# Bringing the first half chunk of x in whole float32 rows on the hardware DMA queues, in a matmul with a decayed running sum

## The chip, the cores and the metric

One core of a Trainium2 chip runs the kernel. The metric is the device time of one execution in microseconds. The core has TensorE (matmuls, "PE" in the profile, its weight loads "PEld"), VectorE (DVE), ScalarE (ACT), GpSimd (POOL) and SyncE (SP). SP and ACT issue DMAs on hardware queues (q1 and q10 in the profile's lists), GpSimd on a software queue (q0). A DMA on GpSimd's queue can change float32 to bfloat16 on the way; here every load on it does.

## The reference

```python
B, S, D = (16, 2048, 1024)      # x is B x S x D, w is D x D, decay has D entries, all float32
xw = x @ w
out[:, 0, :] = xw[:, 0, :]
for t in range(1, S):
    out[:, t, :] = decay[None, :] * out[:, t - 1, :] + xw[:, t, :]
```

It is a matmul of 32768 rows by 1024 x 1024, and then for each of the 1024 output columns a first-order recurrence along time.

## The kernel before

x is cut into 64 chunks of 512 time steps (`TL`), two of which make a group. x has its time steps on rows, while the matmul needs the contracted index on partitions, so each chunk is loaded as bfloat16, turned in blocks of 32 x 32 pairs on VectorE (`turn`, L115), and its even and odd entries are separated by a copy (`part`, L123). The 1024 contracted indices fall into 8 sets k = 2m + e of 128: m from 0 to 3, and e, which says whether the even or the odd entries of x's pairs are meant. Even k can be multiplied straight from the turned pairs (`xw`); odd k take the separated copy (`xt`). For a group, TensorE (`matmul`, L131) computes 8 column tiles n of 128 columns into PSUM; ScalarE, GpSimd and VectorE do the recurrence, VectorE turns the result back (L272) and SP stores it.

The order on every engine is written out by hand: `pin` keeps instructions in program order, and the strings in `agenda` name the work, a letter and a number each. All that the change touches is in the opening, `agenda[-99]`, and in the first matmuls (`step == 0`, L583 to L602). The opening's letters, before the change:

- M0, M1, M2, M3: loads of half chunks of x (chunk 0, first and second half of 256 time steps, then chunk 1), four DMAs each on GpSimd's queue (L105). They are called x0, x1, x2 and x3 below.
- w comes in four quarters, each four DMAs of 32 partitions (`load_w`, L313): the even k of the first 512 columns on SP's and ACT's queues at the very start ("w00"), then on GpSimd's queue U0, the odd k of the same columns ("w01"), and U1 and U2, the same for the other 512 columns.
- W and w, 0 to 15: `settle_one`, the copy of one m of such a quarter from where it landed (`stage`) into the weights `wsb` (L320), W on VectorE and w on ScalarE. 0 to 3 are w00, 4 to 7 are w01.
- E0 to E3: the turns of x0, one m each, on VectorE; E4 to E7 those of x1; E8 to E15 chunk 1's.
- F and G, numbered like E: the separating copies, F on VectorE, G on ScalarE.
- D: the decay values, loaded by SP, turned and squared on VectorE (L367 to L373).
- K0 to K3 and `spin`: matmuls whose result nobody reads. `spin(22, ...)` runs 22 of them from the start; K0 to K3 each copy one element of a landed quarter of x0 into a small tile `gates` on ScalarE (L354) and then run 3, 3, 3 and 2 more with that tile as weights, so that they can't start before the data is there.
- L: a load of a later chunk.

After the opening, step 0 multiplies chunk 0 by the first four column tiles: first the even k of x0 for all four (16 matmuls of 256 columns, k by k), then the even k of x1 (16 more), then the odd k over all 512 columns (16 matmuls), then chunk 1 (the loops from L594). The results lie in `heads`, three PSUM tiles of two banks, whose first banks are `firsts` and second banks `seconds`; `spare` and `spare1` are the fourth pair.

Before chunk 0's results exist, two of the output tiles (`room`) are free, and w's quarters land in them (`stage`, L306).

Of the kernel before, what the change touches and what calls it, by code (L numbers as in the profile page):

```python
# [10 lines left out]
BF16 = mybir.dt.bfloat16  # L11
ALU = mybir.AluOpType


def _ap(ap_obj: bass.AP, new_ap, extra_offset=0):
    return dataclasses.replace(
        ap_obj,
        ap=[list(p) for p in new_ap],
        offset=ap_obj.offset + extra_offset,
    )  # L20
# [5 lines left out]
def kernel(  # L26
# [26 lines left out]
    nc = tc.nc  # L53
    pin = tc.keep_in_program_order
    B, S, D = x.shape
    assert w.shape == (D, D)

    NQ = 4
    P = 32
    CQ = D // NQ  # L60
    K = CQ // P
    M = K // 2
    TL = 512
    NJ = TL // P
    NC = S // TL
    R = K // 2
# [3 lines left out]
    const = ctx.enter_context(tc.tile_pool(name="const", bufs=1))  # L70
    sb = ctx.enter_context(tc.tile_pool(name="sb", bufs=1))
# [4 lines left out]
    def ring(pool, name, count, shape, dtype=FP32):  # L76
        i = turns[name] = turns.get(name, -1) + 1
        return pool.tile(shape, dtype, name=f"{name}{i % count}")

    def quad(q):  # L80
        return slice(q * P, (q + 1) * P)
# [15 lines left out]
    xb_of = {}  # L97
    xw_of = {}
    xt_of = {}
# [25 lines left out]
    def matmul(ps, n, k, xt, t0=0, t1=TL, start=0, pairs=None):  # L125
        if pairs is None:
            rhs = xt[:, k // 2, k % 2, t0:t1]
        else:
            rhs = pairs[:, k // 2, t0 // P:t1 // P, :, k % 2].rearrange("p j i -> p (j i)")
        lhs = wsb[:, k, n].rearrange("p q i -> p (q i)")  # L130
        pin(nc.tensor.matmul(  # L131
            out=ps[:, t0:t1] if ps.shape[1] >= t1 else ps,
            lhsT=lhs,
            rhs=rhs,
            start=(k == 0 and t0 == start),
            stop=(k == K - 1),
        ))
# [3 lines left out]
    class Tile:  # L141
# [39 lines left out]
        def copy(self):  # L181
            self.xs = sb.tile([128, 2 * TL], FP32, name=f"xs{self.lot % 3}")[:, 0:self.T]
            parts = self.ps if isinstance(self.ps, tuple) else (self.ps,)
            size = self.T // len(parts)
            for i, ps in enumerate(parts):
                pin(nc.scalar.copy(out=self.xs[:, i * size:(i + 1) * size], in_=ps))  # L186
# [118 lines left out]
    size = M * CH  # L305
# [5 lines left out]
    def load_w(queues, h, e):  # L311
        for i, q in enumerate((0, 2, 1, 3)):
            pin(queues[i % len(queues)].dma_start(  # L313
                out=stage[h, e][quad(q)].rearrange("p (m d) -> p m d", m=M),
                in_=_ap(w, [[2 * D, P], [2 * P * D, M], [1, CH]],
                        (q * CQ + e) * D + h * CH)))
# [7 lines left out]
    spare = ring(psp, "spare", 1, [128, TL])  # L324
    rows = const.tile([128, 2, P], FP32, name="rows")
    touch = const.tile([128, 1], BF16, name="touch")
    load_w((nc.sync, nc.scalar), 0, 0)
    pin(nc.vector.memset(idle, 0.0))  # L328
    pin(nc.vector.memset(rows, 0.0))
    pin(nc.scalar.copy(out=touch, in_=idle[:, 0:1]))  # L330

    gates = [const.tile([128, 128], BF16, name=f"gate{q}") for q in range(NQ)]
    for gate in gates:
        pin(nc.vector.memset(gate, 0.0))

    def spin(count, by):
        for _ in range(count):
            pin(nc.tensor.matmul(out=spare, lhsT=by, rhs=idle, start=True, stop=True))  # L338

    spin(22, idle[:, 0:128])  # L340
    H = NJ // 2
    halves = ((0, H), (H, NJ))
    for q in range(NQ):
        pin(nc.sync.dma_start(
            out=rows[q * P:q * P + R],
# [3 lines left out]
    def load_half(i):  # L349
        for q in range(NQ):  # L350
            load(i // 2, q, *halves[i % 2])

    def spin_on(q):
        pin(nc.scalar.copy(out=gates[q][quad(q), 0:1], in_=xb_of[0][quad(q), 0, 0:1]))  # L354
        spin(3 if q < NQ - 1 else 2, gates[q])

    def load_part(i):
        load_w((nc.gpsimd,), *((0, 1), (1, 0), (1, 1))[i])
# [21 lines left out]

    ident = const.tile([128, 128], FP32, name="ident")

    def identity(i):
        pin(nc.gpsimd.memset(ident, 0.0))
        pin(nc.gpsimd.affine_select(
            out=ident, in_=ident, compare_op=ALU.not_equal, fill=1.0, base=0,
            pattern=[[-1, 128]], channel_multiplier=1))

    blocks = []
# [45 lines left out]
    def turn_and_load(c):  # L435
# [20 lines left out]
        "F": lambda i: part_one(i, nc.vector.tensor_copy),  # L456
        "G": lambda i: part_one(i, nc.scalar.copy),
        "K": spin_on,
        "D": decays,
        "d": square_again,  # L460
        "I": identity,
# [13 lines left out]
        "L": lambda i: load(*loads.pop(0)) if loads else None,  # L475
    }
    agenda = {
        -99: "M0 M1 U0 M2 M3 U1 U2 w0 W1 w2 W3 K0 K1 K2 K3 E0 E1 G0 E2 G1 E3 F2 G3 E4 E5 G4 E6 G5 E7 F6 G7 W4 w5 W6 W7 D E8 E9 G8 E10 G9 E11 F10 G11 E12 L E13 G12 L E14 G13 E15 L F14 G15",
        0: "p0 z0 W8 W9 W10 W11",
        1: "g0",  # L480
        2: "L S1 L",
# [32 lines left out]
        -19: "p-20 g-20",  # L514
        -18: "j-20 S-19 S-20 k-19 B-19",
        -17: "h-20 k-20 c-20 S-18 k-18",
        -16: "I S-17 B-20 p-16 g-16 j-16",
        -15: "z-15 k-17 B-18 z-16",
        -14: "p-15 g-15 B-17 z-14 j-15",
        -13: "p-14 S-16 g-14 j-14 S-15 h-16 k-16 c-16",  # L520
# [46 lines left out]
            deeds[deed[0]](int(deed[1:] or 0))  # L567

    perform(agenda[-99].split())
    spares = [spare] + [ring(psp, "spare1", 1, [128, TL])]  # L570
    for step, (g, n) in enumerate(slots):
        T = TL * len(g)
        left = step - len(slots)
        if n % R == 0:
            ns, nj = range(n, n + R), T // P
            if left == -2 * R:
                outlets = [Outlet(ns, H, half) for half in range(2)]
            else:
                pieces = 1 if left < -7 * R else 2 if left < -6 * R else nj // H
                outlets = [Outlet(ns, nj, pieces=pieces)]  # L580
        if left == -R:
            outlets = []
        if step == 0:  # L583
            heads = [ring(psp, "ps", 3, [128, T]) for _ in range(3)]
            firsts = [ps[:, 0:TL] for ps in heads] + [spares[0]]
            seconds = [ps[:, TL:T] for ps in heads] + [spares[1]]
            for j0, j1 in halves:
                for k in range(0, K, 2):
                    for i in range(R):
                        matmul(firsts[i], i, k, xt_of[0], j0 * P, j1 * P, pairs=xw_of[0])  # L590
            for k in range(1, K, 2):
                for i in range(R):
                    matmul(firsts[i], i, k, xt_of[0])
            for k0 in range(0, K, 2):  # L594
                for i in range(R):
                    for k in (k0, k0 + 1):
                        matmul(seconds[i], i, k, xt_of[1], 0, H * P,
                               pairs=xw_of[1] if k0 < 4 else None)
            for i in range(R):
                for k in range(K):  # L600
                    matmul(seconds[i], i, k, xt_of[1], H * P, TL, H * P,
                           pairs=xw_of[1] if i < 2 else None)  # L602
        if step < R:
            ps = heads[n] if n < 3 else tuple(spares)
        else:
            if step == K + 1:
                ps = nexts
            elif len(g) == 2 or n % R < 3:
                ps = ring(psp, "ps", 3, [128, T])
            else:  # L610
                ps = ring(psp, "spare", 1, [128, TL])
            todo = [(k, l) for k in range(K) for l in range(len(g))]
            if step < K:
                todo.sort(key=lambda kl: kl[0] % 2)
            elif step == K:
                todo = []
                nexts = (ring(psp, "spare", 1, [128, TL]), ring(psp, "ps", 3, [128, TL]))
                for l in range(len(g)):
                    for i, half in enumerate((ps[:, l * TL:(l + 1) * TL], nexts[l])):
                        for k in range(K):  # L620
                            matmul(half, n + i, k, xt_of.get(g[l]),
                                   pairs=xw_of[g[l]] if g[l] in (3,) else None)
            elif step == K + 1:
                todo = []
            if left == -1:
                ps = tuple(both[:, t:t + TL // 2] for t, both in zip(
                    (0, TL // 2), (ps, ring(psp, "ps", 3, [128, TL]))))
                blocks += [bank("spare1", 1), bank("ps", 3)]
                ends = [(half, k, t) for t, half in zip((0, TL // 2), ps) for k in range(K)]
                advance(K)  # L630
                cross((1,), (0, 1))
                advance(K - 2)
                todo = []
            if 40 <= step < 190:
                pin(nc.tensor.nop(hint="x", nofuse=True))
            for k, l in todo:
                matmul(ps[:, l * TL:(l + 1) * TL], n, k, xt_of[g[l]])
        tiles.append(Tile(g, n, ps, outlets))
        do = agenda.get(step, agenda.get(left) if left >= -20 else None)
        if do is None:  # L640
            do = usual(step)
        else:
            do = do.split()
            if left == -20:
                do = rest(step) + do
        perform(do)
# [29 lines left out]
```

## Time and profile before

| | us |
|---|---|
| median of three runs | 904.14 (904.04, 904.14, 904.42) |
| the profiled execution, from its first to its last instruction (span) | 902.5 |
| what lies around the span, by the median | 1.6 |
| TensorE busy | 896.7 (99%) |
| VectorE busy | 824.2 (91%) |
| ScalarE busy | 686.9 (76%) |
| GpSimd busy | 656.6 (73%) |

The page gives the span of the profiled execution and no other time of it. A busy TensorE is not one at its peak, since matmuls are pipelined; how far it waits is read from the chain of waits and from the timeline. In the timeline a line is: start in us, length in us, engine, line of the kernel, operation, written tile <- read tiles, shapes, how often; in brackets, how long the engine had been idle before and what ended that. In the views by stretches a line is: the stretch, its length, then the busy time and the number of instructions of PE, PEld, DVE, ACT and POOL, the granted TensorE clock, the mean share of the 16 DMA engines that was busy, and the GB/s that they wrote. A line on a DMA queue is: its name and kind, packets, MB written, the time its packets took as a share of 16 engines.

### The profile page before, as it was taken

To read this page: it belongs to the slowest core of one execution; us is meant where nothing else is said; L and a number is where in the kernel's file an instruction comes from. 1 tells how busy PE (TensorE), PEld (TensorE's weight loads), DVE (VectorE), ACT (ScalarE), POOL (GpSimd) and SP (SyncE) were. 2 spreads that over 40 slices of the span, in tenths; PEclk is the share of its full clock that TensorE was granted. 3 is DMA by queue.
4 is the path that set the end of the run, shared out by engine and by line. 5 is a ranking of instruction groups with operands and counts; after the bars stand their busy time and mean duration, and the time that the engine had idled before them with its cause. 6 is when DMAs were issued, how large, how long until landed. Compare 5 with 4: busy or idle time off the path is not lost.

```text
span 902.5 us, 12285 instructions
## 1 busy us (share of the span) xinstructions
PE 896.7 (99%) x4201; PEld 411.4 (46%) x4201; DVE 824.2 (91%) x632; ACT 686.9 (76%) x958; POOL 656.6 (73%) x755
## 2 busy tenths in 40 slices
PE   9999999999999999999999999999999999999998
PEld 5544444444444444444444444444444444444444
DVE  4999998998999999999998999999999999999998
ACT  4889867777877877878778778777787787787743
POOL 7888678777767768777677687777777776876632
PEclk9999999999999999999999999999999999999999
DMA  9999999999999999999999999999999999999858
GB/s 193 194 215 220 231 231 206 215 231 243 251 249 248 242 251 246 244 250 253 227 236 228 221 228 230 232 227 227 232 230 228 227 234 223 228 226 218 183 142 236
DMA packets 403182, 204.77 MB, mean 227 GB/s; under 512 B 9392, under 2 KB 402096, under 8 KB 403120
## 3 DMA queue, kind: packets, MB, share of 16 engines
q1 hardware_dynamic: 265808, 134.77, 60.8%
q0 software_dynamic: 137024, 68.70, 56.8%
q8 instruction: 33, 0.54, 0.2%
q10 hardware_dynamic: 288, 0.52, 0.2%
q14 instruction: 29, 0.24, 0.1%
HBM read 138.42 MB, written 134.22 MB: 302 GB/s over the span
## 4 chain that ended last, share of the span: by engine, by line
PE 98%; DMA 1%; POOL 0%; issue 0%; DVE 0%; DVEq 0%; POOLq 0%
PE ps L131 96%; PE spare L131 1%; DMA xb<-in_x_dram 1%; DMA ot<-in_w_dram 1%; POOL ot L313 0%; PE spare L398 0%; PE ps L398 0%; DVE h L416 0%; DVE wsb L320 0%; DVEq L320 0%; POOLq L660 0%
## 5 line engine op out<-in xcount | busy, mean ns | idle before, releaser
L131 PE MATMUL ps<-xt,wsb 128*128 128x512 bf16 x4016 | 866.1, 378 | 0.5 <-DVE wsb L320 0.5
L131 PEld LDWEIGHTS <-wsb 128*128 128x128 bf16 x4152 | 405.9, 98 | 479.7 <-ACT wsb L320 0.8
L208 POOL TENSOR_TENSOR xs<-h,xs 128x512 f32<-128x512 f32 (+1 forms) x190 | 242.5, 1276 | 187.1 <-ACT h L169 85.5
L186 ACT COPY xs<-ps 128x1024 f32<-128x1024 f32 (+1 forms) x190 | 188.9, 994 | 152.8 <-PE ps L131 147.7
L272 DVE STREAM_TRANSPOSE ot<-so 128x1024 f32<-128x1024 f32 (+2 forms) x264 | 300.1, 1175 | 4.5 <-DMA out_dram<-ot 2.3
L260 POOL TENSOR_TENSOR so<-h,xs 128x512 f32<-128x512 f32 (+1 forms) x190 | 241.1, 1271 | 45.2 <-ACT h L169 28.0
L123 ACT COPY xt<-xw 128x2048 bf16<-128x2048 bf16 (+1 forms) x136 | 242.2, 1789 | 7.8 <-DVE xw L115 7.8
L105 POOL DMA_DIRECT2D xb<-in_x_dram x264 | 174.0, 660 | 3.5 <-DMA ot<-in_w_dram 1.1
L169 ACT ACTIVATE h<-so,dec 128x512 f32<-128x512 f32 (+1 forms) x190 | 145.4, 766 | 29.8 <-DVE so L213 26.7
L115 DVE STREAM_TRANSPOSE xw<-xb 128x2048 f32<-128x2048 f32 (+1 forms) x78 | 147.3, 1900 | 7.0 <-DMA xb<-in_x_dram 7.0
L213 DVE TENSOR_TENSOR_SCAN so<-spare,keep,xs 128x512 f32<-128x512 f32 (+1 forms) x97 | 119.8, 1237 | 25.7 <-POOL xs L208 25.4
L213 DVE TENSOR_TENSOR_SCAN so<-spare,xs 128x512 f32<-128x512 f32 x93 | 113.1, 1218 | 26.5 <-POOL xs L208 23.6
L169 ACT ACTIVATE h<-ps,dec 128x512 f32<-128x512 f32 (+1 forms) x189 | 129.4, 685 | 0.0
L233 DVE TENSOR_TENSOR_SCAN so<-dec,ps 128x1024 f32<-128x1024 f32 x34 | 76.7, 2259 | 1.0 <-ACT h L169 1.0
L233 DVE TENSOR_TENSOR_SCAN so<-dec,keep,ps 128x1024 f32<-128x1024 f32 (+2 forms) x35 | 75.4, 2153 | 0.0
L264 ACT COPY keep<-so 128x1 f32<-128x1 f32 x136 | 25.2, 188 | 9.4 <-DVE so L233 9.0
L204 ACT COPY so<-keep 128x1 f32<-128x1 f32 x97 | 18.5, 192 | 2.7 <-DVE ot L272 2.5
L131 PE MATMUL spare<-xt,wsb 128*128 128x512 bf16 (+1 forms) x56 | 11.9, 341 | 0.0
L131 PE MATMUL ps<-xw,wsb 128*128 128x256 bf16 (+1 forms) x68 | 11.2, 301 | 0.0
L202 POOL MEMSET so<- 128x1 f32 x93 | 10.6, 116 | 0.6 <-DVE ot L272 0.6
L313 POOL DMA_DIRECT2D ot<-in_w_dram x12 | 6.5, 544 | 3.2 <-DMA xb<-in_x_dram 2.1
L338 PE MATMUL spare<-idle 128*128 128x512 bf16 x22 | 7.5, 519 | 1.2 <-DVE idle L328 1.2
(39 smaller groups left out, 39.3 us busy)
## 6 DMA issues: line engine op xcount, KB each, us to landing
out_dram<-ot SPq DMA_DIRECT2D x236, 512.0 KB, 10.9
xb<-in_x_dram POOLq DMA_DIRECT2D x248, 256.0 KB, 7.9
out_dram<-ot SPq DMA_DIRECT2D x56, 128.0 KB, 2.6
xb<-in_x_dram POOLq DMA_DIRECT2D x16, 128.0 KB, 5.8
out_dram<-ot SPq DMA_DIRECT2D x8, 256.0 KB, 4.2
ot<-in_w_dram POOLq DMA_DIRECT2D x12, 128.0 KB, 5.1
out_dram<-xb SPq DMA_DIRECT2D x3, 256.0 KB
ot<-in_w_dram ACTq DMA_DIRECT2D x2, 256.0 KB, 5.1
```

What stands on the lines that cost most here:

```text
L105: pin(nc.gpsimd.dma_start(out=xb_of[c][quad(q), j0:j1], in_=_ap(x, [[D, P], [P * D, j1 - j0], [1, CQ]], (b * S + t0 + j0 * P) * D + q * CQ)))
L115: pin(nc.vector.transpose(out=dst.rearrange("p (m j i) -> p j m i", m=M, i=P)[:, j0:j1, m0:m1], in_=src.rearrange("p (j m c) -> p j m c", ...
L123: pin(copy(out=xt_of[c][:, m0:m1, :, j0 * P:j1 * P], in_=src))
L131: pin(nc.tensor.matmul(out=ps[:, t0:t1] if ps.shape[1] >= t1 else ps, lhsT=lhs, rhs=rhs, start=(k == 0 and t0 == start), stop=(k == K - 1),))
L169: pin(nc.scalar.activation(out=h, in_=src, func=mybir.ActivationFunctionType.Copy, scale=dec[:, self.n:self.n + 1]))
L186: pin(nc.scalar.copy(out=self.xs[:, i * size:(i + 1) * size], in_=ps))
L208: pin(nc.gpsimd.tensor_tensor(out=odds, in0=self.g, in1=odds, op=ALU.add))
L213: pin(nc.vector.tensor_tensor_scan(out=so[:, 3:T + 2:2], data0=squares[-1][:, n:n + 1].to_broadcast([128, T // 2]), data1=self.xs[:, 1:T:2 ...
L233: pin(nc.vector.tensor_tensor_scan(out=so[:, t + 2:t + 2 + size], data0=dec[:, n:n + 1].to_broadcast([128, size]), data1=ps, initial=befor ...
L260: pin(nc.gpsimd.tensor_tensor(out=self.so[:, 2:T + 2:2], in0=self.h, in1=self.xs[:, 0:T:2], op=ALU.add))
L264: pin(nc.scalar.copy(out=self.keep, in_=self.so[:, self.T + 1:self.T + 2]))
L272: pin(nc.vector.transpose(out=outlet.ot[:, :, c0:c0 + P], in_=self.so[:, 2 + t0:2 + t0 + nj * P].rearrange("p (i t) -> p i t", t=P)))
```

## The change

x0 no longer comes through GpSimd's queue. Two DMAs, one on SP's and one on ACT's hardware queue, bring it as float32, each 128 whole rows of 4 KB, into a free part of `room` (`whole`), ahead of w00 on the same queues. GpSimd's queue begins with x1 (M1), and then GpSimd makes a bfloat16 identity `eye` (I0) before it issues w01 (U0).

As whole rows, x0 has time on partitions and all 1024 entries along them. New letters turn it:

- H and J (`gather`): a copy to bfloat16 that picks the even (0, 1) or odd (2, 3) entries of 128 rows in the order of the k sets, H on VectorE, J on ScalarE.
- Q (`erect`): four transposes of 128 x 128 on TensorE into a bank of `seconds`, Q0 and Q1 even entries, Q2 and Q3 odd.
- O and o (`lay`): copies of half of that bank into `xt`, O on ScalarE, o on VectorE; O1 and o0 even entries, O3 and o2 odd.
- N (`begin`): the 16 even-k matmuls of x0 (N0, now from `xt`) and of x1 (N1, from `xw` as before), moved out of step 0 into the opening.

The opening's spins are 12 instead of 22; K0 and K1 now wait for the first and the third piece of w00 instead of pieces of x0, with four spins each, and K2 and K3 are gone, as are E0 to E3, F2, G0, G1 and G3. The identity that the end of the kernel uses is now I1.

```diff
+    H = NJ // 2
+    halves = ((0, H), (H, NJ))
+    whole = room[1][:, size:2 * size].rearrange("p (u c) -> p u c", u=2)
+    for u, queue in enumerate((nc.sync, nc.scalar)):
+        pin(queue.dma_start(out=whole[:, u], in_=_ap(x, [[D, 128], [1, D]], u * 128 * D)))
     load_w((nc.sync, nc.scalar), 0, 0)
...
-    spin(22, idle[:, 0:128])
+    spin(12, idle[:, 0:128])
...
     def spin_on(q):
-        pin(nc.scalar.copy(out=gates[q][quad(q), 0:1], in_=xb_of[0][quad(q), 0, 0:1]))
-        spin(3 if q < NQ - 1 else 2, gates[q])
+        pin(nc.scalar.copy(
+            out=gates[q][0:P, 0:1], in_=stage[0, 0][quad(2 * q), 0:1]))
+        spin(4, gates[q])
+
+    upright = room[0][:, size * 3 // 2:2 * size].bitcast(BF16).rearrange(
+        "p (e u m c) -> p e u m c", e=2, u=2, m=M)
+
+    def gather(i, copy):
+        e, u = i // 2, i % 2
+        pin(copy(out=upright[:, e, u].rearrange("p m (q i) -> p m q i", q=NQ),
+                 in_=whole[:, u].rearrange(
+                     "p (q m i e) -> p e m q i", q=NQ, m=M, e=2)[:, e]))
+
+    def bed(e):
+        return seconds[e].bitcast(BF16).rearrange("p (m t) -> p m t", m=M)
+
+    def erect(i):
+        e, u = i // 2, i % 2
+        for m in range(M):
+            pin(nc.tensor.transpose(
+                out=bed(e)[:, m, u * 128:(u + 1) * 128], in_=upright[:, e, u, m], identity=eye))
+
+    def lay(i, copy):
+        e, m = i // 2, i % 2 * 2
+        if 0 not in xt_of:
+            xt_of[0] = ring(sb, "xt", 5, [128, M, 2, TL], BF16)
+        pin(copy(out=xt_of[0][:, m:m + 2, e, 0:H * P], in_=bed(e)[:, m:m + 2]))
+
+    def begin(i):
+        for k in range(0, K, 2):
+            for n in range(R):
+                if i == 0:
+                    matmul(firsts[n], n, k, xt_of[0], 0, H * P)
+                else:
+                    matmul(firsts[n], n, k, xt_of[0], H * P, TL, pairs=xw_of[0])
...
-        -99: "M0 M1 U0 M2 M3 U1 U2 w0 W1 w2 W3 K0 K1 K2 K3 E0 E1 G0 E2 G1 E3 F2 G3 E4 E5 G4 E6 G5 E7 F6 G7 W4 w5 W6 W7 D E8 E9 G8 E10 G9 E11 F10 G11 E12 L E13 G12 L E14 G13 E15 L F14 G15",
+        -99: "M1 I0 U0 M2 M3 U1 U2 H0 J1 Q0 Q1 H2 J3 O1 o0 K0 K1 w0 W1 w2 W3 N0 Q2 Q3 O3 o2 E4 E5 G4 E6 G5 E7 F6 G7 N1 W4 w5 W6 W7 D E8 E9 G8 E10 G9 E11 F10 G11 E12 L E13 G12 L E14 G13 E15 L F14 G15",
...
         if step == 0:
-            heads = [ring(psp, "ps", 3, [128, T]) for _ in range(3)]
-            firsts = [ps[:, 0:TL] for ps in heads] + [spares[0]]
-            seconds = [ps[:, TL:T] for ps in heads] + [spares[1]]
-            for j0, j1 in halves:
-                for k in range(0, K, 2):
-                    for i in range(R):
-                        matmul(firsts[i], i, k, xt_of[0], j0 * P, j1 * P, pairs=xw_of[0])
             for k in range(1, K, 2):
                 for i in range(R):
                     matmul(firsts[i], i, k, xt_of[0])
```

## The prediction

> **What bounds the kernel now.** I read the page first, then the chain of waits in order of time, then the first 20 us instruction by instruction, then stretches of 1 us for the DMA.
>
> The page's chain that ended last:
>
> ```profile
> PE 98%; DMA 1%; POOL 0%; issue 0%; DVE 0%; DVEq 0%; POOLq 0%
> ```
>
> The same chain in order of time (start, length, what):
>
> ```profile
> 1.31 6.52 DMA xb<-in_x_dram
> ...
> 9.91 4.90 DMA ot<-in_w_dram
> ...
> 14.93 0.30 DVE wsb L320
> 15.23 0.05 issue
> 15.28 0.82 PE ps L131 x3
> ```
>
> What to see: from 15.28 us the chain is TensorE and nothing else until the last transposes at 897.8. Asked for TensorE's waits from 15.3 to 890, the trace gives one, 0.5 us long, and it ends at 15.28. So everything behind the first odd-k matmul is a block of fixed length, and **the time moves by exactly as much as the first odd-k matmul moves from 15.28**. The change touches only what is ahead of it.
>
> The timeline of that stretch:
>
> ```profile
> 1.31 4.70 POOL L105 DMA_DIRECT2D xb<-in_x_dram  x8 [0.86 <-POOLq L660]
> 5.87 0.15 PEld L338 LDWEIGHTS <-idle 128*128 128x128 bf16 x1 [0.28 <-issue]
> 6.29 1.87 PEld L338 LDWEIGHTS <-idle 128*128 128x128 bf16 x9 [0.28 <-issue]
> 7.26 1.14 ACT L320 CAST wsb<-ot 128x512 bf16<-128x512 f32 x2 [4.10 <-DMA ot<-in_w_dram]
> 8.12 0.55 POOL L313 DMA_DIRECT2D ot<-in_w_dram  x1 [2.10 <-DMA xb<-in_x_dram]
> 9.72 1.42 DVE L115 STREAM_TRANSPOSE xw<-xb 128x256 f32<-128x256 f32 x4 [1.66 <-DMA xb<-in_x_dram]
> 10.93 0.50 PE L131 MATMUL ps<-xw,wsb 128*128 128x256 bf16 x3
> 12.35 1.42 DVE L115 STREAM_TRANSPOSE xw<-xb 128x256 f32<-128x256 f32 x4 [0.90 <-DMA xb<-in_x_dram]
> 14.93 0.69 DVE L320 COPY wsb<-ot 128x512 bf16<-128x512 bf16 x3 [0.85 <-DMA ot<-in_w_dram]
> ```
>
> What to see: x's first half chunk ("x0") is usable at 9.7, the second ("x1") at 12.35, w's even k of the first columns ("w00") at 7.3, its odd k ("w01") at 14.9. The even-k matmuls of x0 run from 10.93 to 12.85, those of x1 from 12.85 to 14.82; TensorE then waits 0.46 us for w01. So an earlier x0 alone buys nothing: the last-ending waits are x1 at 12.35 and w01 at 14.9.
>
> Stretches of 1 us (DMA share and GB/s at the end of a line):
>
> ```profile
> 2.00:3.00 1.00, 1.00 (x4) 0.42 (x3) 0.00 (x0) 0.99 (x2) 1.00 (x3) 1.00 0.97 293
> 3.00:4.00 1.00, 1.00 (x4) 0.33 (x3) 0.00 (x0) 0.16 (x1) 1.00 (x3) 1.00 0.94 316
> 4.00:5.00 1.00, 1.00 (x3) 0.30 (x2) 0.00 (x0) 0.00 (x0) 1.00 (x3) 1.00 1.02 289
> 9.00:10.00 1.00, 1.00 (x6) 0.48 (x5) 0.28 (x1) 0.38 (x2) 1.00 (x3) 1.00 1.45 193
> ```
>
> What to see: from 2 to 5 only the two hardware queues move (0.9 MB of w00, 0.30 MB/us); GpSimd's queue, issued from 1.31, shows its first packets only between 5 and 6 (0.10 MB). From then it writes 0.19 to 0.20 MB/us of bfloat16, which is 0.39 MB/us read as float32, without a hole to 20 us. The stream is full from 2 us on.
>
> **The change part by part.** Each of x0, x1, w00, w01 is 1.05 MB in memory.
>
> *Removed from GpSimd's queue:* four issues of x0 (8 took 4.70, so 2.35 us). x1 is issued at 1.31 instead of 3.66, w01 at 1.31 + 2.35 + 0.5 (the new identity; a later row has 0.20 for the memset and 0.29 for the select) = 4.2 instead of 8.12. I cost this at nothing: the 2.10 us wait at 8.12 lay under a full stream, and the same four pieces must still pass before w01 is whole. x0 by 5.5 at 0.30, the other 3.15 MB at 0.39 take 8.1, end 13.6; before, w00 to 5.5 and 3.15 MB the same. x1 at 12.35 and w01 at 14.9 stay, give or take 0.5: a hardware queue that stayed at 0.30 for all of w00 would add 0.8, whole 4 KB rows at 0.39 from the start would take off 0.8.
>
> The Trainium skill, "DMA: Bandwidth & Descriptors", section "Rules for kernel authors", speaks against a gain here: spreading transfers over SP, ACT and GpSimd does not help bandwidth, as all run on the same 16 engines. By it w01 stays at 14.9; by the two rates above it moves by up to 0.8 either way.
>
> *x0 on the hardware queues:* data from 2.0 to 5.5, usable by 6.8 (w00's lag between its last bytes, about 5.5 to 6.4, and its first use, 7.26). Gathers H and J: 0.62 each on ACT (its casts of 512 elements), 0.42 to 0.69 on DVE (its cast, and a 512-element float32 copy out of PSUM, 0.69, at the end of the kernel). Two per engine, eight transposes at 0.11 apart (the float32 ones at the end start 0.11 apart), copies O1 and o0 at about 0.6: done by 9.0. This hides under w00's landing; without that cover it would cost 2.2.
>
> *w00 behind x0 on the same queues: the price of the change.* No row shows it, so I bound it. Unshared at 0.39 from 5.1, 2.7 more, 0.85 to use: 8.7. Shared half by half with x1 (5.4 us) and w00's old lag of 1.7: 5.5 + 5.4 + 1.7 = 12.6. Nearest row, both kinds of queue backlogged, from 44 to 50 us:
>
> ```profile
> q0 software_dynamic: 1271, 0.63, 76.0%
> q1 hardware_dynamic: 1268, 0.64, 52.2%
> ```
>
> Packet for packet, one to one. Here two hardware queues with 2 KB packets stand against one with 1 KB read (512 B written), so w00 gets four fifths of 0.39, 0.31 MB/us: 3.4 us from 5.5, ends 8.9, plus 0.85 = 9.7. I take **9.7**, 2.4 later than before.
>
> *What hangs on w00.* In before this lag would be harmless. In the changed order a straight line hangs on it: w0 (ACT, 0.62 and 0.1 of signalling), 16 matmuls N0 (1.92, as 10.93 to 12.85), eight transposes Q2 Q3 on TensorE (0.88 and 0.25 to the reader), copy o2 on DVE (0.55, between 0.38 of an SBUF copy and 0.69 from PSUM), and only behind o2, in DVE's own order, E4, the first turn of x1 (0.40 and 0.05), then N1 (1.95). Sum 6.7. From 9.7: N0 10.4 to 12.3, o2 done 14.0, E4 14.45, N1 to 16.4. x1, there at 12.35, waits two microseconds behind o2. W4 (0.31) and w5 (0.62) come behind E7 and G7 at 15.4 to 16.7 and are in time for k=1 at 16.4 and k=3 0.86 later. First odd k at 16.4 instead of 15.28: **+1.1 us**.
>
> *Beside the path:* E0 to E3 and F2 off DVE (1.8), G0, G1, G3 (1.66) and two gate copies off ACT, all before 12.85 in waiting time: 0. One more issue on SP and ACT (0.42 each) before the table load, under idle time: 0. The decay rows queue behind 1.05 MB; first read at 15.54, 12 us after their issue: 0. Later, x2 (turned from 17.65) and the second w columns (24.09) keep their stream times while TensorE needs them 1.1 later: no new wait.
>
> *Spins:* 22 become 12: at 0.43 apart they end at 6.5, where the weight loads above change from 0.42 to 0.21 apart. K0 and K1 (8 matmuls, 1.7 at 0.216) wait for the first pieces of w00, about 1 us before the last: under the landing, 0 if the clock holds, else the second rival.
>
> Sum against the profiled execution: 902.5 of span + 1.1 = 903.6; what lies around the span is 904.14 - 902.5 = 1.6 by the median of the three runs, kept: **905.2**.
>
> **The rivals.** What a measurement here tells from no change is 0.2%, 1.8 us.
>
> *A. w00 early (0.15).* Hardware queues are served first, or 4 KB rows run at 0.39: w00 at 8.7, N1 done at 15.4, w01 the limit at 15.2: 904.2, between 903.6 and 904.4. For it: the first 5 us belong to the hardware queues alone. Against: the one-to-one row.
>
> *B. The clock falls: the other side (0.24).* Between the last of 12 spins (6.5) and K0 (about 8.9) TensorE has only eight transposes, 0.9 us of work. Once it slows, K's spins and N0 run at 0.427 and 0.225 apart: 16 x 0.112 = 1.8 on the line: +2.9, 907.0. At the start it took until 6.29 of steady matmuls to be fast; at the end, with the last matmul at 898.4,
>
> ```profile
> 900.00:902.50 2.50, 0.00 (x0) 0.00 (x0) 0.00 (x0) 0.00 (x0) 0.00 (x0) 0.63 0.47 179
> ```
>
> the granted clock averages 0.63 where it was 1.00: idleness of about 2 us can halve it. It decides if the gap between bursts reaches that. Against: the transposes split the gap. The Trainium skill, "TensorE: Matmul & The Clock Gate", Part 1, says an idle window of about 3.4 us throttles the array to half, and Part 4 that transposes don't count as busy; by that the gap is 2.4 to 3 us and the fall hangs on where the window lies. The trace's end agrees that a shorter idle can do it.
>
> *C. Half shares (0.08).* w00 at 12.6: 12.6 + 6.7 - 15.28 = +4.0, 908.2.
>
> *D. It does what it is made for (0.03).* x1 and w01 both come two microseconds earlier because GpSimd starts on x1: N1 done and w01 settled by 13.4, 902.2. Against: the bytes ahead of w01 are the same.
>
> **How the numbers follow.** Forecast 0.50, own range 904.4 to 906.3 (w00 at 8.9 to 10.8); a fifth of it lies above +1.8 (w00 after 10.4). Slower: 0.10 + 0.22 of B + 0.08 = 0.40. Faster: D and a sliver of A, 0.04. Within: 0.56. The range reaches from -0.3 (A) to +3.3 (B with w00 late), 903.8 to 907.4, leaving out C, D and the ends, under 0.2.
>
> **What would show it.** Right: first cast of w (L320) near 9.7; first x0 matmuls near 10.4; DVE's first turn of x1 waiting for TensorE and not for DMA; first odd k near 16.4; w01's copy no longer a wait. Wrong: casts before 8.8 or after 11, spins 0.43 apart again after 8, or w01 landing before 14.

## The result and the profile after

| | before | after |
|---|---|---|
| median, 15 runs each (us) | 904.19 (903.83 to 904.67) | 905.87 (905.66 to 906.76) |
| profiled span (us) | 902.5 | 904.0 |
| first odd-k matmul (us from the span's start) | 15.28 | 16.36 |
| issue of the last store | 899.36 | 900.42 |
| from there to the end of the span | 3.14 | 3.58 |

The changed kernel takes 1.7 us more; the ratio is 1.002, with a 95% interval of 1.0012 to 1.0027. Of the 1.5 us between the two spans, 1.08 lie ahead of the first odd k, where they were forecast, and 0.44 behind the last store, where nothing was forecast. (The spans are given to 0.1 us, so the last row is good to about 0.1.)

The opening of the changed kernel, from its timeline (start, length, engine, line, operation, tiles, and in brackets the idle time before it and what ended it):

```profile
5.51 0.77 DVE L371 CAST ot<-ot 128x512 bf16<-128x512 f32 x2 [4.15 <-DMA ot<-in_x_dram]
...
7.80 1.90 PE L343 MATMUL spare<-idle,gate 128*128 128x512 bf16 x8 [0.76 <-ACT gate L362]
...
10.02 1.14 ACT L320 CAST wsb<-ot 128x512 bf16<-128x512 f32 x2 [1.52 <-DMA ot<-in_w_dram]
...
10.69 0.50 PE L131 MATMUL ps<-xt,wsb 128*128 128x256 bf16 x3 [1.00 <-ACT wsb L320]
...
12.45 0.61 PE L381 MATMUL ps<-eye,ot 128*128 128x128 bf16 x8
...
13.10 0.59 ACT L388 COPY xt<-ps 128x512 bf16<-128x512 bf16 x1 [1.94 <-PE ps L381]
13.71 0.42 DVE L388 COPY xt<-ps 128x512 bf16<-128x512 bf16 x1 [2.76 <-ACT xt L388]
14.06 1.41 DVE L115 STREAM_TRANSPOSE xw<-xb 128x256 f32<-128x256 f32 x4
...
14.54 0.50 PE L131 MATMUL ps<-xw,wsb 128*128 128x256 bf16 x3 [1.48 <-DVE xw L115]
...
15.70 0.72 DVE L320 COPY wsb<-ot 128x512 bf16<-128x512 bf16 x3
...
16.36 0.81 PE L131 MATMUL ps<-xt,wsb 128*128 128x512 bf16 x3
```

x0's first half is usable at 5.5 and its second, on ScalarE, at 5.9, instead of 9.7: about four microseconds earlier, and none of it reaches the end. w00, which now comes behind it, is first cast at 10.0 instead of 7.3. From there the line runs as it was drawn: N0, the transposes of the odd entries, their two copies, x1's turn, x1's even k, first odd k. x1's turn and w01's copies have no wait for a DMA any more; both had one in the kernel before. And o2, the copy on VectorE at 13.71, waits for ScalarE's O3, which the forecast did not have.

The DMA of the changed kernel, by stretches of 1 us:

```profile
3.00:4.00 1.00, 1.00 (x4) 0.32 (x3) 0.00 (x0) 0.63 (x2) 0.98 (x3) 1.00 1.01 406
4.00:5.00 1.00, 1.00 (x3) 0.29 (x2) 0.00 (x0) 0.00 (x0) 0.95 (x3) 1.00 1.03 418
```

and its three queues from 7 to 9 us:

```profile
q10 hardware_dynamic: 168, 0.31, 41.5%
q1 hardware_dynamic: 144, 0.24, 38.9%
q0 software_dynamic: 162, 0.08, 29.8%
```

x0's 4 KB rows move at 0.41 MB/us, where w00's 2 KB pieces, alone on the same queues in the kernel before, moved at 0.30. That the row size makes the difference isn't shown: in a variant below the same 2 KB pieces moved at 0.38. While w00 and x1 are on the engines together, each of the three queues has about the same number of packets: the one-to-one share that the forecast took from the middle of the kernel.

### The profile page after: what moved, and what is told of

The parts are those of the page before. It is cut to its first block, busy times and chain, and to the rows that moved or that the text cites. A ratio compares the mean times of both kernels' runs of the same rounds, so it can differ in the third digit from the quotient of the medians.

```text
span 904.0 us, 12283 instructions
## 1 busy us (share of the span) xinstructions
PE 894.6 (99%) x4204; PEld 410.8 (45%) x4204; DVE 824.0 (91%) x629; ACT 687.1 (76%) x957; POOL 655.5 (73%) x753
## 4 chain that ended last, share of the span: by engine, by line
PE 98%; DMA 1%; ACT 0%; DVE 0%; ACTq 0%; issue 0%; DVEq 0%
PE ps L131 97%; PE spare L131 1%; DMA ot<-in_w_dram 1%; PE spare L442 0%; PE ps L442 0%; DVE h L460 0%; ACT wsb L320 0%; ACT xt L388 0%; PE ps L381 0%; ACTq L313 0%; DVE xw L115 0%; ACTq L331 0%; DVEq L115 0%; DVE xt L388 0%
## 5 line engine op out<-in xcount | busy, mean ns | idle before, releaser
L131 PE MATMUL ps<-xt,wsb 128*128 128x512 bf16 (+1 forms) x4028 | 867.9, 378 | 1.0 <-ACT wsb L320 1.0
L105 POOL DMA_DIRECT2D xb<-in_x_dram x260 | 172.1, 663 | 6.9 <-DMA xb<-in_x_dram 3.9
L131 PE MATMUL ps<-xw,wsb 128*128 128x256 bf16 (+1 forms) x56 | 9.3, 307 | 1.5 <-DVE xw L115 1.5
L343 PE MATMUL spare<-idle 128*128 128x512 bf16 x12 | 4.7, 569 | 1.2 <-DVE idle L333 1.2
```

The costliest lines, as they stand in the source:

```text
L105: pin(nc.gpsimd.dma_start(out=xb_of[c][quad(q), j0:j1], in_=_ap(x, [[D, P], [P * D, j1 - j0], [1, CQ]], (b * S + t0 + j0 * P) * D + q * CQ)))
L131: pin(nc.tensor.matmul(out=ps[:, t0:t1] if ps.shape[1] >= t1 else ps, lhsT=lhs, rhs=rhs, start=(k == 0 and t0 == start), stop=(k == K - 1),))
```

## The experiments

Ten variants were run besides the changed kernel. "First odd k" is read from each one's profile.

| variant | us | kernel before, measured beside it | first odd k | last store's issue to end of span |
|---|---|---|---|---|
| the changed kernel | 905.87 | 904.19 | 16.36 | 3.58 |
| six more small DMAs | 905.43 | 903.95 | 16.36 | 3.17 |
| before, two more small DMAs | 904.44 | 903.95 | 15.05 | 3.57 |
| o2 ahead of O3 | 905.32 | 903.95 | 15.96 | 3.57 |
| x1's turns ahead of o2 | 905.40 | 903.95 | 16.26 | 3.58 |
| both of: x1's turns ahead, six DMAs | 905.13 | 904.27 | 16.18 | 3.16 |
| the same, odd entries in a bank of their own | 904.12 | 904.23 | 15.15 | 3.19 |
| w00 ahead of x0 | 912.13 | 904.27 | 22.83 | 3.51 |
| no K0, K1 | 909.43 | 904.27 | 20.29 | 3.54 |
| x1 held back, identity behind it | 909.41 | 904.23 | 20.15 | 3.49 |
| x1 held back, identity first | 905.25 | 904.39 | 15.85 | 3.46 |

**The end: six more small DMAs in the changed kernel, two more in the kernel before.** SP closes the kernel by waiting for one DMA semaphore after the other. In the built program each store on the hardware queues takes the next of eight semaphores and waits for the DMA eight places before it, so the count of DMAs at the start sets which semaphores the last stores hold.

```diff
+    more = const.tile([128, 2, P], FP32, name="more")
+    for i in range(6):              # in the kernel before: range(2)
+        pin(nc.sync.dma_start(
+            out=more[i * R:i * R + R],
+            in_=_ap(decay, [[P, R], [CH, 2], [1, P]], 0)))
```

> Of the 1.5 us by which the two profiled spans differ, 1.07 lie ahead of the last packet of the last store and 0.43 behind it, in SP's closing waits. Theory 1: the hardware queues' DMAs take eight semaphores in turn, two more DMAs at the start shift the turn by two, and so the last two stores hold the semaphores that SP waits for first and second instead of last; the seven waits left behind them cost 0.06 us each. This kernel is the changed one with six more small DMAs on SP's queue (a second reading of decay into a tile that nobody uses), eight more than before in all, so the turn is the old one: theory 1 expects the gap from the last store's issue to the end of the span to go back by 0.4 us, the first odd-k matmul to stay at 16.4, and 905.4 us in all. Theory 2: the closing difference is chance of one profiled run: 905.9 as the changed kernel, the gap anywhere.

> The kernel before with two more small DMAs on SP's queue (a second reading of decay, unused), and nothing else changed: the turn of the eight semaphores as in the changed kernel. Theory 1 (the closing waits): the head is untouched, first odd-k matmul at 15.3, and the end of the span 0.4 us later behind the last store: 904.6 us. Theory 2 (chance): 904.2, as before.

SP's closing waits in the kernel before, from 901.2 to 902, and in the changed one, from 902.5 to 903.2 (duration in ns, first and last start, count):

```profile
L671 SPq EVENT_SEMAPHORE  x2: 17/22/28, 901.6 to 901.9; - x2
```

```profile
L713 SPq EVENT_SEMAPHORE  x7: 28/28/28, 902.7 to 903.1; - x7
```

What SP waited for at its end, before and then after:

```profile
SPq L671 <- DMA out_dram<-xb: 0.6, 1, 0.6
SPq L671 <- DMA out_dram<-h: 0.6, 1, 0.6
```

```profile
SPq L713 <- DMA out_dram<-xb: 1.1, 1, 1.1
...
SPq L713 <- DMA out_dram<-h: 0.6, 1, 0.6
```

Before, the last DMA wait, at 901.6, is one of the two in its line, and the engines' closing signal follows. After, the first of the seven, at 902.7, is the wait that the last store's landing ends; six more stand behind it to 903.1, none of them for anything still open, 0.06 us apart. In the built program the last two stores' semaphores stand eighth and ninth of nine waits before, second and third after, so six are left behind them, one fewer than the theory counted. The gap from the last store to the end of the span is 3.14 before, 3.58 changed, 3.17 with six more DMAs in the changed kernel, and 3.57 with two more in the kernel before, whose head is not touched. The first theory holds in both directions; the cost is 0.4 us. It is read from the gaps. The whole times go the same way, +0.5 for the two DMAs alone and +1.5 for the changed kernel with the turn restored, where the gaps give +0.4 and +1.2, but they settle less: the ratio for the two DMAs alone is 1.0005, with an interval from 0.9996 to 1.0014, and times compare to some 0.2 us (in this variant of before, w01 was copied 0.2 earlier and the first odd k came at 15.05).

**o2 ahead of O3.**

```diff
-        -99: "... N0 Q2 Q3 O3 o2 E4 E5 ..."
+        -99: "... N0 Q2 Q3 o2 O3 E4 E5 ..."
```

> The changed kernel with o2 ahead of O3 in the written order. In the changed kernel's trace VectorE's copy o2 waits for ScalarE's copy O3 from the same PSUM bank, 0.6 us, though neither needs the other's result, and the turn of x1 waits behind o2. Theory 1 (the line from w's landing through o2 to x1's turn sets the first odd k): o2 runs 0.6 us earlier and O3 after it, x1's first turn starts near 13.5 instead of 14.06, first odd k at 15.8, 905.3 us. Rival: the odd k's weights w01 or the copies G on ScalarE, which now stand 0.4 later behind O3, are the next limit: then the first odd k moves by less than 0.3 and the time stays at 905.6 to 905.9.

```profile
13.17 0.42 DVE L388 COPY xt<-ps 128x512 bf16<-128x512 bf16 x1 [2.14 <-PE ps L381]
13.51 1.41 DVE L115 STREAM_TRANSPOSE xw<-xb 128x256 f32<-128x256 f32 x4
13.63 0.58 ACT L388 COPY xt<-ps 128x512 bf16<-128x512 bf16 x1 [2.40 <-DVE xt L388]
```

Now ScalarE waits for VectorE: whichever copy comes first in the written order, the other waits, so the two never read that bank together. x1's turn starts 0.55 earlier, as the theory has it, and the first odd k comes at 15.96, 0.4 earlier, where 0.55 was expected; the first three of x1's matmuls take 0.65 here against 0.50.

**x1's turns ahead of o2, alone and with the end's repair.**

```diff
-        -99: "... Q2 Q3 O3 o2 E4 E5 G4 E6 G5 E7 F6 G7 N1 ..."
+        -99: "... Q2 Q3 O3 E4 E5 G4 E6 G5 E7 o2 F6 G7 N1 ..."
```

> The changed kernel with the four turns of x1 ahead of o2 in VectorE's order. Theory 1: x1 has landed by about 12.5 and its turn then starts at its landing instead of at 14.06; the even-k matmuls of x1 follow the last transposes at 13.1, end at 15.1, and the first odd k, which now waits for o2 and the settled w01, comes at 15.2 to 15.5: 904.8 us (the end's 0.4 stays). Rival: x1 lands only near 14 because its bytes went behind w's on the shared engines; then turn and first odd k stay where they are, 905.9 us.

> Both repairs in the changed kernel: x1's turns ahead of o2, and six more small DMAs so that the closing waits stand in the old order. If the two costs are the whole of the loss and independent, the time is that of the kernel before within 0.3 us: 904.3 us, first odd k at 15.2 to 15.5. If it lies 0.5 us or more above, something else of the change costs time; if it lies below 903.9, x0's early arrival is worth something once nothing waits behind o2.

```profile
12.29 1.42 DVE L115 STREAM_TRANSPOSE xw<-xb 128x256 f32<-128x256 f32 x4 [0.96 <-DMA xb<-in_x_dram]
...
13.26 0.28 PE L131 MATMUL ps<-xw,wsb 128*128 128x256 bf16 x1
...
14.08 0.42 DVE L388 COPY xt<-ps 128x512 bf16<-128x512 bf16 x1 [0.37 <-ACT xt L388]
...
14.56 0.39 PE L131 MATMUL ps<-xw,wsb 128*128 128x256 bf16 x2 [1.02 <-DVE xt L388]
```

x1 lands at 12.29, against 12.35 in the kernel before, so the rival (x1 only near 14) falls. But the theory's gain does not come: one of x1's matmuls starts at 13.26, and the second waits for o2 until 14.56. With the end's repair added the time is 0.86 above before, and 0.9 is also what the first odd k, at 16.18, is late. Part of the gain is hidden: w00 was first cast at 10.38 and 10.31 in these two profiles instead of 10.02, and from that cast to the first odd k it is 5.9 us instead of 6.34. But the microsecond that the theory gave is not there; something else tied these matmuls to o2.

**The odd entries in a bank of their own.**

```diff
     def bed(e):
-        return seconds[e].bitcast(BF16).rearrange("p (m t) -> p m t", m=M)
+        return seconds[3 * e].bitcast(BF16).rearrange("p (m t) -> p m t", m=M)
```

> Turning x1 ahead of o2 gained only 0.1 to 0.2 us: x1's turn began at 12.3, but the second of x1's even-k matmuls then waited 1.0 us for o2 itself. Reading of that: the odd entries are transposed into the second bank of a PSUM tile whose first bank these matmuls write, and the write waits until o2 has read the other bank. This kernel is the one with both repairs (x1's turns ahead of o2, six more small DMAs), and the odd entries are transposed into the bank that belongs to no such tile (spare1). If the reading is right, x1's even k run from 13.1 or 13.2 without a hole to 15.1, the first odd k comes at 15.1 to 15.4, limited by w01's landing at 14.9, and the time is that of the kernel before within 0.3 us: 904.2. If the wait has another cause (TensorE behind ScalarE's O3, or VectorE's own order), the hole stays and the time is 0.9 above before, 905.1.

```profile
10.98 0.50 PE L131 MATMUL ps<-xt,wsb 128*128 128x256 bf16 x3 [0.93 <-ACT wsb L320]
...
12.44 1.42 DVE L115 STREAM_TRANSPOSE xw<-xb 128x256 f32<-128x256 f32 x4 [1.19 <-DMA xb<-in_x_dram]
...
12.74 0.61 PE L386 MATMUL spare<-eye,ot 128*128 128x128 bf16 x8
13.19 0.50 PE L131 MATMUL ps<-xw,wsb 128*128 128x256 bf16 x3
...
14.80 0.70 DVE L320 COPY wsb<-ot 128x512 bf16<-128x512 bf16 x3
...
15.15 0.82 PE L131 MATMUL ps<-xt,wsb 128*128 128x512 bf16 x3
```

The hole is gone, the first odd k comes at 15.15, and the time is 904.12 against 904.23: a ratio of 0.9998, from 0.9989 to 1.0007. `seconds[1]`, the bank used by the change, is the second bank of the PSUM tile whose first bank x1's second matmul writes; the program made that write wait for o2's read of the other bank. So there were two ties to o2, VectorE's order and the shared PSUM tile, and the second hid most of what cutting the first gains. (The bank alone was not changed in any run; that the first tie would hide the second likewise is read from the changed kernel, where x1's turn itself stood behind o2 until 14.06.) With both cut and the closing waits turned back, the whole loss is gone, and x0's arrival four microseconds earlier is still worth nothing. The reason is w00: TensorE starts N0 at 10.98, behind w00's first cast at 10.31 and no earlier than in the kernel before (10.93), and from there has work without a hole, the transposes and x1's even k, until the first odd k could start at 15.0. It starts 0.15 later, behind w01's first copy at 14.80. That copy has no wait for a DMA, as it had in the kernel before; it stands behind o2 and F6 in VectorE's order.

**Is w00 late by sharing?** GpSimd's first load of x1 is held back until x0 has landed.

```diff
     def load_half(i):
+        if i == 1:
+            pin(nc.gpsimd.tensor_copy(out=late, in_=whole[:, 0, 0:1]))
...
-        -99: "M1 I0 U0 ..."
+        -99: "I0 M1 U0 ..."     # second form only
```

> The changed kernel with GpSimd's first load (x1) held back until x0 has landed, by a one-column copy out of x0 on GpSimd ahead of it; its packets then start near 9.5 instead of 6.0. Theory (w00 is late by what it shares with x1, 0.2 MB read as float32 by 9.0): the first cast of w comes at 9.2 to 9.5 instead of 10.0; x1 lands at 13.5 to 14.3 and w01 at 16.5 to 17, and the first odd k, now waiting for w01, at 17 to 17.5: 906.6 us. Rival (w00's lateness comes from being second alone, the sharing costs nothing): the first cast stays at 10.0.

> The same as the run before, with the identity made ahead of GpSimd's wait: in that run the identity stood behind x1's four issues, TensorE's first transposes waited for it until 9.1, and ScalarE's cast of w, in order behind them, began at 11.1 whenever w had landed. Its packets had the two hardware queues empty at 8.5, where the changed kernel has them empty at 9.5. Theory (w00 is late by what it shares with x1): first cast of w near 9.0 to 9.3 instead of 10.0; x1's turn near 13.5, w01's copies near 15.5 to 16.5, first odd k at 16 to 17, 905.5 to 906.6 us, as what w00 gains x1 and w01 lose. Rival (sharing costs nothing, w00 is late by coming second): first cast at 10.0.

The first form missed (909.41): the identity was late, so TensorE was idle from 5.6 to 9.1, the granted clock fell to 0.50 from 8 us on, and the casts stood in order behind the transposes' copies. In the second form, the queues from 6 to 7 us, from 7 to 8, and then first cast and first odd k:

```profile
q1 hardware_dynamic: 109, 0.19, 55.0%
q10 hardware_dynamic: 107, 0.19, 53.0%
```

```profile
q10 hardware_dynamic: 113, 0.20, 54.8%
q0 software_dynamic: 78, 0.04, 29.2%
q1 hardware_dynamic: 103, 0.08, 26.2%
```

```profile
9.11 1.14 ACT L320 CAST wsb<-ot 128x512 bf16<-128x512 f32 x2 [1.40 <-DMA ot<-in_w_dram]
...
15.50 0.70 DVE L320 COPY wsb<-ot 128x512 bf16<-128x512 bf16 x3 [0.63 <-DMA ot<-in_w_dram]
15.85 0.82 PE L131 MATMUL ps<-xt,wsb 128*128 128x512 bf16 x2 [0.24 <-DVE wsb L320]
```

With x1 started two microseconds later w00 moves at 0.38 MB/us and is cast 0.9 earlier, inside what the theory of sharing gave. (The other profiles with x0 ahead of w00 and x1 undelayed have this cast at 10.02 to 10.38, so the 0.9 is clear of their spread.) It is still 1.85 later than in the kernel before, which is the price of coming second and of what x1 still shares from 7.7 us on. x1's turn comes earlier by as much, and w01, which pays for it, lands at 15.5 and is now the limit: the first odd k at 15.85, 0.5 earlier than in the changed kernel and 0.6 later than before. That and the 905.25 lie just below the ranges given (16 to 17, 905.5 to 906.6).

**w00 ahead of x0.**

```diff
+    load_w((nc.sync, nc.scalar), 0, 0)
     for u, queue in enumerate((nc.sync, nc.scalar)):
         pin(queue.dma_start(out=whole[:, u], in_=_ap(x, [[D, 128], [1, D]], u * 128 * D)))
-    load_w((nc.sync, nc.scalar), 0, 0)
```

> The changed kernel with the two queue positions swapped: w's even k ahead of x0 on the hardware queues. Theory (the price is what comes second on the hardware queues): the first cast of w falls back to 6.5 to 7.3 and x0 lands near 10 instead of w; its gather, transposes and copies (about 2 us) then stand on the line, N0 starts near 12.3 and the first odd k comes near 18: 907.4 us. Rival (the price is the shared DMA stream, whatever the order): no change, 905.9.

The direction was right and the size wrong by 4.7 us. x0 was usable at 11.4 and not near 10, and the first cast of w, put at 6.5 to 7.3, came at 13.95, since ScalarE and VectorE have it behind x0's copies in their order. TensorE was idle from 6.5 to 11.9, and the clock fell to 0.50 for the eight matmuls of K0 and K1, which took 3.6 us and stood ahead of N0 (17.15). The written order puts K behind x0's copies, so this run shows more than the price of the second place and does not give that price alone.

**No K0 and K1.**

```diff
-        -99: "... O1 o0 K0 K1 w0 W1 ..."
+        -99: "... O1 o0 w0 W1 ..."
```

> The changed kernel without K0 and K1, so TensorE has only eight transposes between the 12 spins (to 5.9) and N0 (10.7). Theory: idleness of that length halves the clock, N0's 16 matmuls then start 0.22 apart instead of 0.11, 1.8 us more on the line: first odd k near 18, 907.6 us, and the mean granted clock lower than 0.999. Rival (the clock holds, or N0 waits for w anyway and the casts are the limit): 905.9 us, first odd k at 16.4.

Stretches of this run (PEclk is the third number from the end):

```profile
6.00:10.00 4.00, 1.27 (x10) 0.50 (x8) 1.14 (x3) 1.74 (x3) 0.48 (x1) 1.00 1.15 265
10.00:14.00 4.00, 2.94 (x14) 2.09 (x15) 0.76 (x2) 1.14 (x2) 3.16 (x6) 0.50 1.32 199
14.00:17.00 3.00, 1.52 (x13) 1.21 (x11) 0.84 (x3) 0.62 (x2) 2.59 (x5) 0.50 1.44 193
17.00:20.30 3.30, 3.30 (x17) 2.25 (x17) 3.22 (x13) 2.56 (x5) 2.73 (x5) 0.51 1.39 196
```

With only the eight transposes between 6.5 and 11 the clock is at half from 10 us until the first odd k at 20.29. Rival B of the forecast is a real mechanism, and K0 and K1 are what keeps it off; of the 3.9 us by which the head is longer (16.36 to 20.29), 0.36 are a later w00 (first cast at 10.38) and 3.6 are the clock's price. The forecast had 1.8, because it slowed N0 alone (+1.6 here); the transposes (+0.45) and x1's matmuls (+1.5) are slow as well.

## Why the prediction was right or wrong

It put the time at 905.2 in 903.8 to 907.4, most likely within 0.2% of before, a little slower. Measured: 905.87, 1.7 us slower, inside the range and just inside the 1.8 us.

- *The time moves as the first odd k moves.* Right, with the limit below: the chain behind that matmul has the same length in both kernels (15.28 to the last store's issue at 899.36 is 884.08, and 16.36 to 900.42 is 884.06). In all twelve profiles this stretch is 884.06 to 884.16.
- *First odd k at 16.4.* It came at 16.36, partly by errors that cancel. The first cast of w was put at 9.7 and came at 10.02. From that cast to the first odd k the sum had 6.7, and the profile has 6.34: the eight transposes took 0.65 to their reader and not 1.13, x1's even k 1.82 and not 1.95, N0 1.76 and not 1.92, and o2 0.35 and not 0.55, while o2's wait for O3 added 0.6 that the sum did not have.
- *x0 hidden under w00's landing.* Right: usable at 5.5 to 5.9, earlier than the 6.8 forecast, since its bytes moved at 0.41 and not 0.30 MB/us; laid out by 8.1, two microseconds ahead of the cast of w.
- *w00's place and share.* Right in mechanism. The one-to-one share shows in the queues from 7 to 9 us, and starting x1 later moved the cast from 10.02 to 9.11.
- *The stream stays full, so x1 and w01 do not move.* Right in the landings: x1 at 12.29 where a variant let its turn start at the landing, and w01's first copy at 14.94 in the variant of the changed kernel with both repairs, where it waited for the DMA. But the reason is in part luck: the stream of the changed kernel was not full throughout. Counting GpSimd's bytes as read, it moved 0.16 MB from 2 to 3 us and 0.24 from 6 to 7, where the kernel before moved 0.29 and 0.32; x0's 0.41 from 3 to 5 made up for it, and by 10 us both had moved about 2.7 MB. Two errors of opposite sign, for each of which the forecast allowed up to 0.8 us, cancelled. The rule of the Trainium skill's page "DMA: Bandwidth & Descriptors" that was weighed there (more issuing engines give no bandwidth) agrees with these landings.
- *"Only behind o2, in DVE's own order, E4."* This step failed as an explanation, though its time was right. Taking E4 out of that order gained 0.1 at the first odd k (0.5 counted from w00's cast); the shared PSUM tile held x1's matmuls at nearly the same place. Only cutting both gained the microsecond.
- *"What lies around the span ... kept", and "the block of fixed length" to the end.* This is the term that was missing: 0.4 us of closing waits. It was put at nothing because the change touches only the opening; but two more DMAs on the hardware queues turn the semaphores under all later stores. Head 1.08 and end 0.44 make the 1.5 of the spans; the medians differ by 1.68, and the remaining 0.2 is not more than the kernel before's own first odd k moved between two profiles (15.05 and 15.28). What lies around the span was kept, but mis-sized: the sum had 1.6, from a median and the span of another execution, and in every execution that has both on record it is 1.73 to 1.86. The span forecast, 903.6, with 0.4 for the closing waits and 1.8 around it gives 905.8. So the 0.7 us by which 905.2 was short are mostly those two terms.
- *Rivals.* B did not happen in the profile, whose granted clock is 1.00 in every stretch of the opening; of the fifteen runs one, at 906.76, has a mean clock of 0.997 where the others have 0.999 or 1.000. The run without K shows the mechanism. In the changed kernel the opening spins end at 5.86 and K0's begin at 7.80; an estimate from the windows of 3.41 us in the last section is that any window over this gap held at least 1.5 us of spins, where 1.1 was too little with x1 held back (first form). The reading that about 2 us of idleness can halve the clock counts from the last transpose at 898.4; from the last ordinary matmul, which ends at 897.1, to the fall of the clock at 900.66 it is 3.6 us, and the run that shows a fall after 2.3 us is the first form of x1 held back (last section). A (w00 at 8.7) and C (at 12.6) are excluded by the cast at 10.02, and D (two microseconds gained) by the landings of x1 and w01.

## What to carry to other kernels

When several loads share a full stream, ask which one ends the last wait and not which one comes early: here x0 came four microseconds sooner, w00 had to come later for it, and the copies ordered behind w00 lengthened the line. If moving an instruction out of a suspected line gains little, look for a second tie at the same place (here a PSUM tile shared by two banks' users) before dropping the suspicion. And a change at the start can reach the very end through anything that is handed out in turn, such as DMA semaphores; compare the tail of the two traces as well as the head.

## What was not expected of the hardware

- SP's closing waits cost 0.06 us each even when nothing is open: six of them behind the last landing made 0.4 us.
- On the two hardware queues together, loads in 4 KB rows wrote 0.41 MB/us (3 to 5 us), and loads in 2 KB pieces 0.30 from 2 to 5 us in the kernel before but 0.38 from 6 to 7 with x1 held back, all float32 from memory and with nothing on GpSimd's queue. What slowed the pieces in the first of these is open.
- GpSimd's first packets came about 4 us after its first issue or later at the start of both kernels (issue at 1.31, none before 5.2 and 5.8), and about 2 us after it (5.71 to 7.7) in the variant that issued later. Why is open; no run tells it.
- Once halved, the granted clock stayed at half for ten microseconds in the run without K0 and K1, although TensorE was busy for 7.8 of 10.3 us (10 to 20.3), with two holes of 1 us or more. The moments at which it fell and rose, 9.98 and 20.22 there, 7.87 and 14.69 in the first form of x1 held back, 10.36 and 17.19 with w00 ahead of x0, lie 10.24, 6.82 and 6.83 us apart: three, two and two times 3.41. The Trainium skill, "TensorE: Matmul & The Clock Gate", Part 1, has the clock lifted by a whole busy window of about 3.4 us, and the windows running freely, not from the first matmul. The runs agree with such windows, but the one that lifts the clock need not be busy from end to end: the last of the three in the run without K had matmuls for 3.2 us of its 3.41 (16.98 to 20.22), the first for 2.3 (11.05 to 13.39), and that one left the clock at half. Nor need the one that halves it be idle: in the first form of x1 held back it held 1.1 us of spins (to 5.55), so that the clock fell after 2.3 us of idleness. Where between these values the limits lie, no run shows.
